# Batched top-k by token tile, tree sums, split low parts and wide late up blocks in a three-layer expert network

## The chip, the cores and the metric

The kernel runs on one NeuronCore of a Trainium2 chip. The metric is the device time of one execution in microseconds (us): 3051.55 is the median of three runs of the kernel before (3051.2 to 3052.03). TensorE (PE) multiplies matrices, VectorE (DVE) and ScalarE (ACT) work elementwise, GpSimd (POOL) and SyncE (SP) here mostly start DMAs. Each engine runs its own instructions in a fixed order and waits on semaphores.

## What is computed

256 tokens of width 1024 pass three blocks. Each block has a mixer (convolution and a recurrence; chunked linear attention; stick-breaking attention) and then an expert layer, `peer_ffn`, which takes most of the time and is what the change touches:

```
q = (xb @ w_q).reshape(TOK_BLOCK, PEER_HEADS, 2, PEER_DHALF)
s = jnp.einsum('thcd,hcnd->thcn', q, sub_keys).astype(jnp.float32)
top_s, top_i = lax.top_k(s, K)                       # K = 16 of 128 keys, 8 heads x 2 halves
cand = top_s[:, :, 0, :, None] + top_s[:, :, 1, None, :]
best_s, best_c = lax.top_k(cand.reshape(TOK_BLOCK, PEER_HEADS, K * K), K)
i1 = jnp.take_along_axis(top_i[:, :, 0], best_c // K, axis=-1)
i2 = jnp.take_along_axis(top_i[:, :, 1], best_c % K, axis=-1)
e = (i1 * PEER_NKEYS + i2).reshape(TOK_BLOCK, PEER_HEADS * K)
gate = jax.nn.softmax(best_s, axis=-1).reshape(TOK_BLOCK, PEER_HEADS * K)
u = expert_u[e]
act = jax.nn.gelu(jnp.einsum('td,ted->te', xb, u), approximate=False)
coef = (gate * act.astype(jnp.float32)).astype(xb.dtype)
return jnp.einsum('te,ted->td', coef, expert_v[e])
```

## The kernel before

The kernel gathers no experts. It computes the activation of all 16384 experts for all tokens ("up"), multiplies by a dense matrix of gates that is zero for experts not chosen, and multiplies by all of `expert_v` ("down"). Both loops run over 128 blocks of 128 experts.

**Weights in two parts.** `stream` (L72) loads a 128x1024 fp32 block into `raw` (four buffers), ScalarE makes `hi`, its value in the matmul format (L79), VectorE makes `lo = raw - hi` (L81); three buffers each of `hi` and `lo`. `mm3` (L109) multiplies as hi x hi, hi x lo, lo x hi, three matmuls for one product. The activations are stored in two parts as well, `xh` and `xl`, in two tiles.

**`peer` (L1049), one layer.** First the query loop: 16 blocks of `wq`, each with its scores (L1158) against the keys, which ScalarE copies into `S`. Then the up loop (L1189): a block is 8 x `mm3`, 24 matmuls of 256 columns into the PSUM tile `pu`, of which there are four, and a Gelu by ScalarE into the SBUF tile `C` (L1197). Then the down loop (`vstep`, L1208): 12 matmuls of 512 columns a block, with `ch` and `cl`, the two parts of `C` times gate.

**Work in the background.** The top-k of the scores, mostly VectorE's, is written as a generator (`background`, L1082) that yields its declared cost after each piece; `pull(rate)` (L1143), called once per query block from the third on and once per up block, takes pieces for a budget of 1.5. Before the change the pieces come in this order: rankings of all 32 score rows (`topk1`, both token tiles by turns), `topk2` of token tile 0 for its eight heads (rank the sums of the two halves, Exp, decode the rank into two indices, look up with 16 compare-and-multiply steps and four reduces, L1293 and L1300), 128 indirect DMAs that write tile 0's gates to the DRAM tensor `G` (L1097), `topk2` of tile 1, and the spread: for each four tokens of tile 1 VectorE and ScalarE build one-hot rows `A` and `B`, and eight recorded matmuls (L1131) make their dense gates `pg`, which multiply `C`. Gates for up blocks not yet done are put into `C` first, and the Gelu's result is then multiplied in (L1201).

**Buffers.** The scratch of the top-k lies in the last part of `C` (from block NS on). Tag "A" of the pool `wp` has two buffers: the one-hot tile `A` of the spread, then the tile `gate` of the down loop, into which POOL reads tile 0's gates from `G` for four blocks at a time (L1211); VectorE multiplies them into `C` (L1214).

**Order.** A scheduler in the framework orders each engine's instructions from the program text and dependencies; `issue_after` (L100, L1143) keeps an instruction behind a given `lo`.

Of the kernel before, what the change touches and what calls it, by code (L numbers as in the profile page):

```python
# [6 lines left out]
F32 = mybir.dt.float32  # L7
# [32 lines left out]
class Net:  # L40
# [31 lines left out]
    def stream(self, ap, n=1024):  # L72
# [7 lines left out]
        with self.behind():  # L80
            self.los.append(nc.vector.tensor_tensor(lo, raw, hi.bitcast(F32), op=OP.subtract))  # L81
# [172 lines left out]
    def block1(self, a, xh_out, xl_out, stop=None):  # L254
# [5 lines left out]
        with ExitStack() as ctx:  # L260
# [7 lines left out]
            xh = self.xp.tile([128, 8, 272], F32R, tag="xh", name="xh1")  # L268
            xl = self.xp.tile([128, 8, 272], F32R, tag="xl", name="xl1")
# [779 lines left out]
    def peer(self, xh, xl, wq, skT, uT, v, G, Gnext=None, rate=1.5, dve_a=2):  # L1049
# [7 lines left out]
        NS = 88  # L1057
        with ExitStack() as ctx:
# [9 lines left out]
            tmp = scr(1024, 5120)  # L1068
            small = [scr(1920, 6144 + 1920 * i) for i in range(2)]
            cand = [scr(512, 512 * i) for i in range(2)]  # L1070
            eq = scr(4096, 1024)
# [10 lines left out]
            def background():  # L1082
                for g in range(16):
                    for tt in range(2):
                        yield from self.topk1(views[tt], S[tt], tmp, 2 * g + tt)
                yield from self.topk2(views[0], cand[0], tmp, eq)
                pick = views[0]["pick"]
                idx = wp.tile([128, 128], U32, tag="idx", name="idx", bufs=1)
                gts = wp.tile([128, 128], F32, tag="gts", name="gts", bufs=1)
                V.tensor_copy(gts, pick[:, 2])  # L1090
                V.tensor_scalar(pick[:, 0], pick[:, 0], 128.0, self.col, op0=OP.mult, op1=OP.add)
                V.scalar_tensor_tensor(pick[:, 0], pick[:, 1], 16384.0, pick[:, 0], op0=OP.mult, op1=OP.add)
                V.tensor_copy(idx, pick[:, 0])
                for h in range(8):
                    now = []
                    for k in range(16 * h, 16 * h + 16):
                        i = nc.gpsimd.indirect_dma_start(  # L1097
                            G, bass.IndirectOffsetOnAxis(ap=idx[:, k:k + 1], axis=0), gts[:, k:k + 1], None,
                            compute_op=OP.add)
                        for j in now:  # L1100
                            tc.declare_no_dep(i.ins, j.ins, reason="distinct experts of a head")
# [333 lines left out]
```

## Time and profile before

| | |
|---|---|
| median of 3 runs | 3051.55 us |
| profiled execution | 3049.45 us, its span 3047.6 us |
| PE busy | 2973.8 us, 98% |
| DVE busy | 2077.3 us, 68% |
| ACT busy | 1619.5 us, 53% |
| POOL busy | 865.6 us, 28% |
| DMA | 568.80 MB, mean 187 GB/s |

The span runs from the first to the last instruction; 1.85 us lie around it. The up loops begin at 346, 1308 and 2278 us and the down loops at 750, 1713 and 2684 us; each down loop takes 348 us. What stands between is the mixers and the query loops. A share over the whole span hides the stages, so the rows further down are taken by stretch.

### The profile page before, as it was taken

How to read it: one execution, taken by the hardware profiler on the slowest of the kernel's cores; microseconds unless marked ns; L12 is line 12 of the kernel's file. 1: busy time of each engine (PE TensorE's matmuls, PEld its weight loads, DVE VectorE, ACT ScalarE, POOL GpSimd, SP SyncE). 2: the span in 40 equal slices, each digit the busy share in tenths (PEclk: the TensorE clock that was granted, in tenths of full speed). 3: DMA queues.
4: the chain of work that ended last, by engine and by line, in shares of the span. 5: the costliest groups of instructions: out<-in, count | busy, mean ns of one | idle time of the engine just before them, and what ended most of it. 6: DMA issues, size and time to landing. Idle time of an engine off the chain costs nothing.

```text
span 3047.6 us, 55671 instructions
## 1 busy us (share of the span) xinstructions
PE 2973.8 (98%) x21313; PEld 2719.7 (89%) x21313; DVE 2077.3 (68%) x4439; ACT 1619.5 (53%) x3016; POOL 865.6 (28%) x564
## 2 busy tenths in 40 slices
PE   9999999999999999999999999998999999999998
PEld 8888999999888888899999988887889999988886
DVE  6976997545666665798744566665599864466666
ACT  6345558544444454456844544446544774454443
POOL 0000057784000010008788100000002777800000
PEclk9999999999999999999999999999999999999999
DMA  9735566666676653456666666664345666666665
GB/s 312 238 131 202 174 167 139 167 184 194 217 218 218 217 185 118 157 175 158 138 182 183 204 218 217 218 214 164 119 156 173 151 147 185 182 215 217 216 217 177
DMA packets 231915, 568.80 MB, mean 187 GB/s; under 512 B 74416, under 2 KB 99264, under 8 KB 231392
## 3 DMA queue, kind: packets, MB, share of 16 engines
q1 hardware_dynamic: 165536, 529.31, 53.4%
q0 software_dynamic: 66112, 35.94, 8.3%
q8 instruction: 167, 2.74, 0.4%
q14 instruction: 100, 0.82, 0.1%
HBM read 533.49 MB, written 31.65 MB: 185 GB/s over the span
## 4 chain that ended last, share of the span: by engine, by line
PE 87%; DVE 9%; ACT 2%; issue 1%; DMA 1%; POOL 0%; DVEq 0%; ACTq 0%; SPq 0%; POOLq 0%
PE pu L113 11%; PE py L164 11%; PE py L162 11%; PE py L163 11%; PE pu L112 11%; PE pu L111 11%; PE pg L1131 3%; DVE lo L81 2%; PE pz L113 2%; PE pz L111 2%; PE pz L112 2%; DVE acc L340 1%; PE pq L113 1%; PE pq L112 1%; PE pq L111 1%
## 5 line engine op out<-in xcount | busy, mean ns | idle before, releaser
L81 DVE TENSOR_TENSOR lo<-raw,hi 128x1024 fp32r<-128x1024 f32 (+1 forms) x939 | 1142.6, 1218 | 762.6 <-ACT hi L79 757.3
L79 ACT CAST hi<-raw 128x1024 fp32r<-128x1024 f32 (+1 forms) x939 | 979.9, 1045 | 1192.5 <-issue 725.7
L1097 POOL DMA_INDIRECT G<-gts,idx x384 | 782.3, 2037 | 532.0 <-DVE gts L1090 236.3
L113 PE MATMUL pu<-xh,lo 128*128 128x256 f32 x3072 | 873.9, 284 | 7.7 <-DVE lo L81 7.7
L111 PE MATMUL pu<-xh,hi 128*128 128x256 f32 x3072 | 878.3, 286 | 3.0 <-ACT hi L79 3.0
L112 PE MATMUL pu<-xl,hi 128*128 128x256 f32 x3072 | 870.5, 283 | 0.0
L113 PEld LDWEIGHTS pu<-xh,lo 128*128 128x128 f32 x3072 | 590.2, 192 | 12.4 <-DVE lo L81 11.0
L162 PE MATMUL py<-hi,ch 128*128 128x512 f32 x1536 | 598.0, 390 | 0.0
L163 PE MATMUL py<-lo,ch 128*128 128x512 f32 x1536 | 597.1, 389 | 0.0
L164 PE MATMUL py<-hi,cl 128*128 128x512 f32 x1536 | 597.0, 389 | 0.0
L111 PEld LDWEIGHTS pu<-xh,hi 128*128 128x128 f32 x3072 | 590.3, 192 | 3.6 <-ACT hi L79 3.6
L112 PEld LDWEIGHTS pu<-xl,hi 128*128 128x128 f32 x3072 | 590.5, 192 | 0.0
L162 PEld LDWEIGHTS py<-hi,ch 128*128 128x128 f32 x1536 | 288.3, 188 | 61.4 <-ACT ch L106 1.9
L164 PEld LDWEIGHTS py<-hi,cl 128*128 128x128 f32 x1536 | 288.3, 188 | 61.1 <-DVE cl L107 1.4
L163 PEld LDWEIGHTS py<-lo,ch 128*128 128x128 f32 x1536 | 288.3, 188 | 59.5
L1211 POOL DMA_DIRECT2D gate<-G x96 | 51.9, 541 | 993.1 <-DVE C L1214 971.1
L107 DVE TENSOR_TENSOR cl<-C,ch 128x256 fp32r<-128x256 f32 x384 | 160.9, 419 | 4.4 <-ACT ch L106 4.4
L106 ACT CAST ch<-C 128x256 fp32r<-128x256 f32 x384 | 152.7, 398 | 12.9 <-DVE C L1214 12.9
L111 PE MATMUL pz<-xh,hi 128*128 128x256 f32 (+1 forms) x504 | 150.9, 301 | 7.9 <-ACT hi L79 5.5
L113 PE MATMUL pz<-xh,lo 128*128 128x256 f32 (+1 forms) x504 | 148.8, 296 | 1.0 <-DVE lo L81 1.0
L112 PE MATMUL pz<-xl,hi 128*128 128x256 f32 (+1 forms) x504 | 148.1, 294 | 0.1
L1197 ACT ACTIVATE C<-pu 128x128 f32<-128x128 f32 (+13 forms) x384 | 119.3, 312 | 0.2
(490 smaller groups left out, 3546.7 us busy)
## 6 DMA issues: line engine op xcount, KB each, us to landing
raw<-in_u_dram SPq DMA_DIRECT2D x384, 512.0 KB
raw<-in_v_dram SPq DMA_DIRECT2D x384, 512.0 KB
G<-zero SPq DMA_DIRECT2D x96, 256.0 KB
raw<-in_wq_dram SPq DMA_DIRECT2D x48, 512.0 KB
gate<-G POOLq DMA_DIRECT2D x96, 256.0 KB
raw<-in_w_in_dram SPq DMA_DIRECT2D x38, 512.0 KB
raw<-in_a_w_inT_dram SPq DMA_DIRECT2D x14, 512.0 KB
raw<-in_b_wT_dram SPq DMA_DIRECT2D x14, 512.0 KB
```

The source lines that it names most:

```text
L79: nc.scalar.copy(hi, raw)
L81: self.los.append(nc.vector.tensor_tensor(lo, raw, hi.bitcast(F32), op=OP.subtract))
L106: nc.scalar.copy(hi, src)
L107: nc.vector.tensor_tensor(lo, src, hi.bitcast(F32), op=OP.subtract)
L111: mm(out, lh, rh, start=start, stop=False)
L112: mm(out, lh, rl, start=False, stop=False)
L113: mm(out, ll, rh, start=False, stop=stop)
L162: mm(po[q], xh[:, ts], hi[:, h], start=f, stop=False)
L163: mm(po[q], xh[:, ts], lo[:, h], start=False, stop=False)
L164: mm(po[q], xl[:, ts], hi[:, h], start=False, stop=l)
L1097: i = nc.gpsimd.indirect_dma_start(G, bass.IndirectOffsetOnAxis(ap=idx[:, k:k + 1], axis=0), gts[:, k:k + 1], None, compute_op=OP.add)
L1197: nc.scalar.activation(C3[:, b, :tm], pa[:, :tm], AF.Gelu)
```

## The change

Five edits, all but the fourth inside `peer` and its helpers.

1. Top-k by token tile and by batches of four heads. `background` becomes two lists of jobs; each has the number of score rows that it needs, and `pull` takes the first list whose head may run, tile 0's before tile 1's. `topk2` runs on four heads and is called four times a layer; the scatter goes out in two halves; the scratch is smaller and starts at block 84 in place of 88.
2. In `topk2` the 16 lookup products are summed by a tree of adds in place of the reduces.
3. After the last job, up blocks take `hi` against both parts of x in one 512-column matmul, then `lo` against `xh`. The two halves of the PSUM tile are then added: ScalarE copies one out into a tile `sum` (tag "A"), VectorE adds the other, and the Gelus read `sum`.
4. `lo` is made in two halves of 512 elements, in every stream.
5. For that `xh` and `xl` become one tile with both parts of a chunk side by side.

```diff
--- before.py
+++ after.py
@@ -78,7 +78,10 @@
         lo = self.sp.tile([128, n], F32R, tag="lo", name="lo")
         nc.scalar.copy(hi, raw)
         with self.behind():
-            self.los.append(nc.vector.tensor_tensor(lo, raw, hi.bitcast(F32), op=OP.subtract))
+            for i in range(0, n, 512):
+                p = slice(i, min(i + 512, n))
+                sub = nc.vector.tensor_tensor(lo[:, p], raw[:, p], hi[:, p].bitcast(F32), op=OP.subtract)
+            self.los.append(sub)
         return hi, lo
 
     def chore(self, n):
@@ -265,8 +268,8 @@
                 s = VO1[name]
                 return vec[:, s] if i is None else vec[:, s.start + i:s.start + i + 1]
 
-            xh = self.xp.tile([128, 8, 272], F32R, tag="xh", name="xh1")
...
+    def peer(self, xh, xl, xx, wq, skT, uT, v, G, Gnext=None, rate=1.5, dve_a=2):
...
-        NS = 88
+        NS = 84
...
+            def scatter(hf):
+                K = slice(64 * hf, 64 * hf + 64)
...
+                for h in range(4 * hf, 4 * hf + 4):
...
+            jobs = [[], []]
+            for tt in range(2):
+                for hf in range(2):
+                    for g in range(8 * hf, 8 * hf + 8):
+                        jobs[tt].append((g + 1, self.topk1(views[tt], S[tt], tmp, 2 * g + tt)))
+                    jobs[tt].append((8 * hf + 8, self.topk2(views[tt], cand, tmp, eq, 4 * hf)))
+                    if tt == 0:
+                        jobs[tt].append((8 * hf + 8, scatter(hf)))
+            jobs[1].append((16, spread()))
+            debt, now_ = [0.0], [None]
+
+            def pull(budget, scored=16):
...
                 debt[0] += budget
                 with tc.issue_after(self.los[-PACE].ins):
                     while debt[0] > 0:
-                        c = next(bg, None)
+                        if now_[0] is None:
+                            q = next((q for q in jobs if q and q[0][0] <= scored), None)
+                            if q is None:
+                                debt[0] = 0.0
+                                return
+                            now_[0] = q.pop(0)[1]
+                        c = next(now_[0], None)
                         if c is None:
-                            return False
-                        debt[0] -= c
-                return True
+                            now_[0] = None
+                        else:
+                            debt[0] -= c
...
                 if g > 1:
-                    pull(rate)
+                    pull(rate, g - 1)
...
-                for c in range(8):
-                    s = slice(c * 128, c * 128 + 128)
-                    self.mm3(pa[:, :256], hi[:, s], lo[:, s], xh[:, c], xl[:, c], c == 0, c == 7)
+                src = pa
+                if any(jobs) or now_[0]:
+                    for c in range(8):
+                        s = slice(c * 128, c * 128 + 128)
+                        self.mm3(pa[:, :256], hi[:, s], lo[:, s], xh[:, c], xl[:, c], c == 0, c == 7)
+                else:
+
+                    for c in range(8):
+                        s = slice(c * 128, c * 128 + 128)
+                        nc.tensor.matmul(pa, hi[:, s], xx[:, c].rearrange("p x n -> p (x n)"), start=c == 0, stop=False)
+                    for c in range(8):
+                        s = slice(c * 128, c * 128 + 128)
+                        nc.tensor.matmul(pa[:, 256:], lo[:, s], xh[:, c], start=False, stop=c == 7)
+                    src = wp.tile([128, 256], F32, tag="A", name="sum")
+                    nc.scalar.copy(src, pa[:, 256:])
+                    with tc.issue_after(self.los[-1].ins):
+                        V.tensor_tensor(src, src, pa[:, :256], op=OP.add)
                 tm = state["tok"]
-                nc.scalar.activation(C3[:, b, :tm], pa[:, :tm], AF.Gelu)
+                nc.scalar.activation(C3[:, b, :tm], src[:, :tm], AF.Gelu)
...
-        for h in range(8):
+        for h in range(4):
...
         for j in range(16):
-            V.scalar_tensor_tensor(r16(e2[:, j]), r16(cf.rearrange("p c n -> p (c n)")), float(j),
-                                   tj[:, :, j, None].to_broadcast([128, 16, 16]), op0=OP.is_equal, op1=OP.mult)
+            V.scalar_tensor_tensor(e[:, j], cfn, float(j), tj[:, :, j, None].to_broadcast([128, 8, 16]),
+                                   op0=OP.is_equal, op1=OP.mult)
...
-        for i in range(4):
-            N = slice(i * 64, i * 64 + 64)
-            V.tensor_reduce(pick[:, 0:2].rearrange("p c n -> p (c n)")[:, N], e3[:, N], axis=AX.X, op=OP.add)
-            yield 1.1
...
+        for n in (1024, 512, 256):
+            V.tensor_tensor(eq[:, :n], eq[:, :n], eq[:, n:2 * n], op=OP.add)
+            if n > 256:
+                yield 0.0012 * n
+        V.tensor_tensor(pick[:, 0:2], eq[:, 0:128].rearrange("p (c n) -> p c n", c=2),
+                        eq[:, 128:256].rearrange("p (c n) -> p c n", c=2), op=OP.add)
```

Three places show how the engines' orders move. Numbers behind a name tell one buffer from another; a block's `raw`, `hi`, `lo` and `pu` carry near numbers.

TensorE at the end of the first layer's up loop, before: the last matmuls of block 127 and the first of down.

```order
L112 MATMUL pu_9849<-xl_97,hi_9845 128x256
L113 MATMUL pu_9849<-xh_96,lo_9846 128x256
L111 MATMUL pu_9849<-xh_96,hi_9845 128x256
L112 MATMUL pu_9849<-xl_97,hi_9845 128x256
L113 MATMUL pu_9849<-xh_96,lo_9846 128x256
L162 MATMUL py_9878<-hi_9886,ch_9891 128x512
L163 MATMUL py_9878<-lo_9887,ch_9891 128x512
L164 MATMUL py_9878<-hi_9886,cl_9892 128x512
```

The same place now, the last three up blocks:

```order
L1224 MATMUL pu_9780<-x_96,hi_9775 128x512 x8
L1227 MATMUL pu_9780<-x_96,lo_9776 128x256 x8
L1224 MATMUL pu_9811<-x_96,hi_9806 128x512 x8
L1227 MATMUL pu_9811<-x_96,lo_9807 128x256 x8
L1224 MATMUL pu_9842<-x_96,hi_9837 128x512 x8
L1227 MATMUL pu_9842<-x_96,lo_9838 128x256 x8
L165 MATMUL py_9866<-hi_9874,ch_9880 128x512
L166 MATMUL py_9866<-lo_9875,ch_9880 128x512
L167 MATMUL py_9866<-hi_9874,cl_9881 128x512
```

A block is now eight wide matmuls on `hi` and then eight narrow ones on `lo`, where 24 narrow ones went round `hi`, `hi`, `lo`. Of the 128 blocks of each layer, 74 keep the old form and 54 have the new one; the first of these follows the last `pg` matmul of the spread.

ScalarE at the same place, before, from the `hi` of block 127 on:

```order
L79 CAST hi_9845<-raw_9843 128x1024
L1197 ACTIVATE C_3873<-pu_9744 128x128
L1200 ACTIVATE act_9770<-pu_9744 128x128
L79 CAST hi_9886<-raw_9884 128x1024
L1197 ACTIVATE C_3873<-pu_9779 128x128
L1200 ACTIVATE act_9805<-pu_9779 128x128
L106 CAST ch_9891<-C_3873 128x256
L79 CAST hi_9909<-raw_9907 128x1024
L1197 ACTIVATE C_3873<-pu_9814 128x128
L1200 ACTIVATE act_9840<-pu_9814 128x128
L106 CAST ch_9914<-C_3873 128x256
L1197 ACTIVATE C_3873<-pu_9849 128x128
```

and now, from the `hi` of the first down block on:

```order
L79 CAST hi_9874<-raw_9872 128x1024
L1229 COPY sum_9797<-pu_9780 128x256
L1233 ACTIVATE C_3925<-sum_9797 128x128
L1236 ACTIVATE act_9801<-sum_9797 128x128
L79 CAST hi_9898<-raw_9896 128x1024
L1229 COPY sum_9828<-pu_9811 128x256
L1233 ACTIVATE C_3925<-sum_9828 128x128
L1236 ACTIVATE act_9832<-sum_9828 128x128
L79 CAST hi_9922<-raw_9920 128x1024
L1229 COPY sum_9859<-pu_9842 128x256
L1233 ACTIVATE C_3925<-sum_9859 128x128
L1236 ACTIVATE act_9863<-sum_9859 128x128
```

Each block's two Gelus now stand behind a copy and read `sum`, which VectorE has to add up first; `hi` of the block three further on stands ahead of a block's Gelus in both.

VectorE in the same stretch, before:

```order
L81 TENSOR_TENSOR lo_9846<-raw_9843,hi_9845 128x1024
L1201 TENSOR_TENSOR C_3873<-C_3873,act_9770 128x128
L81 TENSOR_TENSOR lo_9887<-raw_9884,hi_9886 128x1024
L1201 TENSOR_TENSOR C_3873<-C_3873,act_9805 128x128
L1214 TENSOR_TENSOR C_3873<-C_3873,gate_9882 128x128
L107 TENSOR_TENSOR cl_9892<-C_3873,ch_9891 128x256
L81 TENSOR_TENSOR lo_9910<-raw_9907,hi_9909 128x1024
L1201 TENSOR_TENSOR C_3873<-C_3873,act_9840 128x128
L1214 TENSOR_TENSOR C_3873<-C_3873,gate_9882 128x128
L107 TENSOR_TENSOR cl_9915<-C_3873,ch_9914 128x256
```

and now:

```order
L83 TENSOR_TENSOR lo_9899<-raw_9896,hi_9898 128x512
L1231 TENSOR_TENSOR sum_9828<-sum_9828,pu_9811 128x256
L83 TENSOR_TENSOR lo_9899<-raw_9896,hi_9898 128x512
L1237 TENSOR_TENSOR C_3925<-C_3925,act_9832 128x128
L83 TENSOR_TENSOR lo_9923<-raw_9920,hi_9922 128x512
L1231 TENSOR_TENSOR sum_9859<-sum_9859,pu_9842 128x256
L83 TENSOR_TENSOR lo_9923<-raw_9920,hi_9922 128x512
L1237 TENSOR_TENSOR C_3925<-C_3925,act_9863 128x128
L1250 TENSOR_TENSOR C_3925<-C_3925,gate_9870 128x128 x3
L110 TENSOR_TENSOR cl_9881<-C_3925,ch_9880 128x256
L110 TENSOR_TENSOR cl_9905<-C_3925,ch_9904 128x256
L110 TENSOR_TENSOR cl_9929<-C_3925,ch_9928 128x256
```

The add into `sum` stands between the two halves of a later block's `lo`. The multiplies by `gate` used to alternate with the last multiplies by `act`; now three of them stand behind all of these, with three `cl` after them. The DMA that fills `gate_9870` takes a buffer of tag "A", in which `sum` was before.

## Rows read from the trace of the kernel before

**Rows 1.** The page's part 1: busy us, share of the span, instructions.
```profile
PE 2973.8 (98%) x21313; PEld 2719.7 (89%) x21313; DVE 2077.3 (68%) x4439; ACT 1619.5 (53%) x3016; POOL 865.6 (28%) x564
```

**Rows 2.** Busy us (x instructions) of PE, PEld, DVE, ACT, POOL; granted clock; DMA.
```profile
560.00:747.00 187.00, 187.00 (x1561) 187.00 (x1560) 92.85 (x132) 89.48 (x195) 137.94 (x59) 1.00 0.67 186
760.00:1095.00 335.00, 335.00 (x1478) 276.87 (x1477) 217.07 (x370) 166.53 (x247) 15.80 (x30) 1.00 0.69 216
```

**Rows 3.** The same view, first up block to first gate matmul, three layers.
```profile
346.20:451.30 105.10, 101.07 (x827) 99.42 (x826) 101.59 (x322) 53.81 (x83) 38.74 (x21) 1.00 0.63 177
1307.60:1414.40 106.80, 103.45 (x828) 101.15 (x827) 103.21 (x330) 53.87 (x84) 38.48 (x19) 0.98 0.61 177
2277.50:2385.00 107.50, 104.14 (x831) 101.70 (x830) 103.94 (x331) 54.40 (x85) 38.54 (x19) 0.98 0.61 177
```

**Rows 4.** VectorE's groups by shape: count | busy us, mean ns | idle before.
```profile
L107 DVE TENSOR_TENSOR cl<-C,ch 128x256 fp32r<-128x256 f32 x384 | 160.9, 419 | 4.4 <-ACT ch L106 4.4
L1214 DVE TENSOR_TENSOR C<-C,gate 128x128 f32<-128x128 f32 x384 | 109.3, 285 | 0.0
L1293 DVE SCALAR_TENSOR_TENSOR C<-C 128x256 f32<-128x256 f32 x96 | 33.7, 418 | 0.2
```

**Rows 5.** VectorE in order of time, lookup sums: start us, us, instruction.
```profile
1395.76 1.22 DVE L81 TENSOR_TENSOR lo<-raw,hi 128x1024 fp32r<-128x1024 f32 x1
1396.90 1.98 DVE L1300 TENSOR_REDUCE C<-C 128x64 f32<-128x1024 f32 x1
1398.80 1.22 DVE L81 TENSOR_TENSOR lo<-raw,hi 128x1024 fp32r<-128x1024 f32 x1
```

**Rows 6.** ScalarE in order of time at the second Exp of layer 2.
```profile
1374.74 1.05 ACT L79 CAST hi<-raw 128x1024 fp32r<-128x1024 f32 x1 [1.55 <-PE pu L112]
...
1376.09 1.28 ACT L1270 ACT_TABLE_LOAD   x1
1381.34 0.31 ACT L1270 ACTIVATE C<-C 128x128 f32<-128x128 f32 x1 [3.96 <-DVE C L1269]
1381.66 1.28 ACT L1197 ACT_TABLE_LOAD   x1
```

**Rows 7.** ScalarE in order of time, one late up block of layer 1.
```profile
741.83 1.05 ACT L79 CAST hi<-raw 128x1024 fp32r<-128x1024 f32 x1 [1.49 <-PE pu L112]
742.78 0.27 ACT L1197 ACTIVATE C<-pu 128x128 f32<-128x128 f32 x1
742.95 0.27 ACT L1200 ACTIVATE act<-pu 128x128 f32<-128x128 f32 x1
```

**Rows 8.** TensorE in order of time where up ends, layer 1.
```profile
750.27 0.28 PE L113 MATMUL pu<-xh,lo 128*128 128x256 f32 x1
750.39 0.40 PE L162 MATMUL py<-hi,ch 128*128 128x512 f32 x1
```

**Rows 9.** POOL in order of time: the last add to G, the first gates.
```profile
719.94 2.57 POOL L1097 DMA_INDIRECT G<-gts,idx  x1 [0.30 <-issue]
727.00 1.20 POOL L1211 DMA_DIRECT2D gate<-G  x2 [4.49 <-DVE lo L81]
756.48 0.54 POOL L1211 DMA_DIRECT2D gate<-G  x1 [28.28 <-DVE C L1214]
```

**Rows 10.** POOL in order of time where one head's writes follow another's.
```profile
437.47 1.54 POOL L1097 DMA_INDIRECT G<-gts,idx  x1 [0.31 <-issue]
441.82 1.54 POOL L1097 DMA_INDIRECT G<-gts,idx  x1 [2.81 <-issue]
```

**Rows 11.** Busy by stretch around TensorE's wait that ends at 2082.32.
```profile
2080.00:2083.20 3.20, 0.87 (x6) 0.63 (x7) 3.20 (x6) 0.96 (x3) 0.53 (x1) 1.00 0.76 234
2083.40:2086.60 3.20, 3.08 (x14) 2.58 (x13) 3.20 (x8) 0.79 (x2) 0.35 (x1) 0.50 0.95 334
```

**Rows 12.** TensorE's waits: us in total, times, longest.
```profile
PE ptr L199 <- DVE res L722: 12.4, 5, 3.4
...
PE pz L113 <- DVE lo L81: 5.3, 3, 2.3
```

More of the change, by code (lines that the diff above doesn't have):

```diff
@@ L1067, in peer @@
             S = [scr(2048, 2048 * i).rearrange("p (g n) -> p g n", n=128) for i in range(2)]
[L1068 to L1071, printed above, removed]
+            tmp = scr(1024, 4096)
+            small = [scr(1920, 5120 + 1920 * i) for i in range(2)]
+            eq = scr(2048, 8960)
+            cand = scr(256, 11008)
             views = [self.topk_views(s_) for s_ in small]
@@ L1080, in after, with gates @@
                     tc.add_manual_dep(i.ins, j.ins.name, SYNC, reason="adds of the head before")
[L1082 to L1093, printed above, removed]
-                for h in range(8):
[L1095 to L1101, printed above, removed]
-                        after(i)
-                        now.append(i)
-                    last[:] = now
-                yield 0.8
-                yield from self.topk2(views[1], cand[1], tmp, eq)
-                pick = views[1]["pick"]
-                pt = self.ps.tile([128, 512], F32, tag="y", name="pt", bufs=4)
-                for i in range(3):
-                    nc.tensor.transpose(pt[:, i * 128:i * 128 + 128], pick[:, i], self.ident)
-                idT = wp.tile([128, 5, 128], F32, tag="idT", name="idT", bufs=1)
-                nc.scalar.copy(idT[:, 0:3].rearrange("p a b -> p (a b)"), pt[:, :384])
-                V.tensor_scalar(idT[:, 3], idT[:, 0], -1.0, None, op0=OP.mult)
-                V.tensor_scalar(idT[:, 4], idT[:, 2], -1.0, None, op0=OP.mult)
-                yield 1.0
+            def gates():
                 for t0 in range(252, 127, -4):
@@ new lines, in spread @@
+            def spread():
+                pick = views[1]["pick"]
+                pt = self.ps.tile([128, 512], F32, tag="y", name="pt", bufs=4)
+                for i in range(3):
+                    nc.tensor.transpose(pt[:, i * 128:i * 128 + 128], pick[:, i], self.ident)
+                nc.scalar.copy(idT[:, 0:3].rearrange("p a b -> p (a b)"), pt[:, :384])
+                V.tensor_scalar(idT[:, 3], idT[:, 0], -1.0, None, op0=OP.mult)
+                V.tensor_scalar(idT[:, 4], idT[:, 2], -1.0, None, op0=OP.mult)
+                yield 1.0
+                yield from gates()
@@ L1261, in topk2 @@
             V.tensor_tensor(c3[:, :, o:o + n * nb].rearrange("p h (a b) -> p h a b", b=nb),
[L1262 to L1265 removed]
+                            tv4[:, :, 0, a0:a1, None].to_broadcast([128, 4, n, nb]),
+                            tv4[:, :, 1, None, 0:nb].to_broadcast([128, 4, n, nb]), op=OP.add)
+        yield 0.9
+        for h in range(4):
             self.top16(bv[:, h], bi[:, h], c3[:, h], tmp[:, h * 64:h * 64 + 64])
@@ L1390, in xt @@
         def xt():
-            return [n.xp.tile([128, 8, 256], F32R, tag="x" + x, name="x" + x) for x in "hl"]
+            t = n.xp.tile([128, 8, 2, 256], F32R, tag="x", name="x")
+            return t[:, :, 0], t[:, :, 1], t
         def peer(l, x):
```

83 lines of the change are left out of this document (48 added, 35 removed).

## The prediction

> **What bounds the kernel now.** I read the page's busy table first: TensorE is busy for 98% of the span, VectorE for 68% [rows 1]. Then stretches with one kind of work. In the late up stretch 1561 matmuls of 256 columns fill 187 us, 119.8 ns each; in the down stretch 1478 of 512 columns fill 335 us, 226.7 ns each [rows 2]. A column at the full clock (2.4 GHz) takes 0.4167 ns, so 256 and 512 columns are 106.7 and 213.3 ns, and both kinds carry the same 13 ns on top: a fixed price per matmul. There TensorE never waits.
>
> It does wait early in each up loop, while VectorE does the top-k. The three stretches from the first up matmul to the first matmul of the gate spread last 105.1, 106.8 and 107.5 us with 827, 828 and 831 matmuls [rows 3]. At 119.8 ns these are 99.1, 99.2 and 99.6 us, so 6.0, 7.6 and 7.9 us are lost: 21.5 us in all. VectorE is busy there for 97% of the time.
>
> Two things lose them. VectorE's starts show what an instruction really occupies: a `lo` of 1024 elements 1.14 us (1395.76 to 1396.90) though its record says 1.22, a reduce of L1300 1.90 us [rows 5]; a record is some 0.083 longer than the step to the next start. A reduce and a `lo` come to 3.04 us, against a block of 24 x 0.1198 = 2.875 us. And the Exp of the second top-k keeps ScalarE from 1376.09, when its table load starts, to 1381.65, of which 3.96 us waiting for VectorE, and a second table load follows; no `hi` is made meanwhile [rows 6].
>
> **The change part by part.** *Late up blocks.* From the first block after the spread, 54 of 128 blocks of each layer, 162 in all, replace 24 matmuls of 256 columns by 8 of 512 and 8 of 256. The columns stay 6144. 8 x 226.7 + 8 x 119.8 = 2772 ns against 2875: 0.103 us less per block, **-16.7 us** for 162.
>
> The Trainium skill (TensorE: Matmul & The Clock Gate, "Back-to-back issue gap") gives N/2.4 + 2.5 ns at the full clock. By that rule eight matmuls fewer are worth an estimated 20 ns a block, 3.2 us in all. The trace disagrees: 13 ns each.
>
> *What the wide blocks add.* A ScalarE copy out of PSUM (0.4 us), a VectorE add (0.42 us, as the 256-element L107 [rows 4]), and a longer way round: ScalarE makes `hi` of block b+3, copies b, waits for the add of b, does two Gelus; VectorE does the first half of `lo` of b+3, the add, the second half. In that order ScalarE's round is `hi` 1.05, first half of `lo` 0.60 (half of 1.14 plus half of the fixed part), add 0.42, Gelus 0.17 each by their starts (742.78, 742.95) [rows 7], hops about 0.1: 2.5 us. That is below 2.77, so TensorE stays the bound and this costs nothing; `hi` is two blocks early, so a slower round would first eat some 5 us of lead per layer.
>
> *Top-k.* The 48 rankings of a layer stay. By starts, lookups were 32 of 256 elements (0.335 us) and 8 reduces (1.90): 25.9 us; now 64 of 128 (0.20) and trees of 1024, 512, 256 and 128 elements, 4 times (1.14 + 0.60 + 0.34 + 0.20): 21.9 us. The small steps at half length, twice as often, give about 4 us back: a fixed 0.07 us each [rows 4, 5]. In the up stretches VectorE's busy time, 101.6 to 103.9 us, less 35 `lo` of 1.14 leaves 62 to 64 us of this background [rows 3], 1.77 us per block or more. The rate of 1.5 per block against declared costs (72.8 a layer before, 86.4 now) hands the work out in 49 portions before (14 in the query loop, 35 up blocks) and 58 now (14 and 44). So the layer's background is 49 x 1.77 = 86 us, before and, by the two sums just made, still. Per portion with its `lo`: before 1.77 + 1.14 = 2.91 us, over the block's 2.875; now 86/58 + 1.20 = 2.68, under it. Late then: the Exp. There are four a layer, one in the query loop, three in the up loop (before two). With VectorE under its limit each should find it about one `lo` behind, a delay that the two-block lead takes up. Bounds: all 21.5 us go; or each of three Exps costs what the worst costs now (some 3.7 us by the arithmetic of rows 3 and 6, where 7.6 us hold two), 11 per layer, +12. I take **-13**: a little remains at each Exp and at the start of the spread, which looks the same in both orders.
>
> The spread starts eight or nine blocks later; it is 32 x 8 matmuls wherever it stands: nothing.
>
> *Where up hands over to down.* Before, the first down matmul starts 0.12 us after the last up matmul [rows 8], since the first gate pair was read long before. Now the buffers of tag A hold the sums of up blocks to the end: `gate` of the first down blocks takes the buffer of block 126's sum, and POOL waits for its last Gelu. That one is over 1.85 us after block 126 ends (copy, half a `lo`, add, two Gelus), 0.9 us before 127 ends. Then comes the gate's issue, 0.54 us [rows 9], and its landing. No row shows a gate's landing; the nearest are POOL's writes to G, where a new head started 4.35 us after the start of the issue before it, 2.81 us after its end [rows 10]. So 3.35 us, then the multiply (0.29) and the cast `ch` (0.4) with hops: TensorE stands still for about 3.4 us. Behind that multiply VectorE holds two more, three `cl` and the next `lo`, all for down; POOL holds only the next gate, wanted four blocks later. (G itself is long written: its last add was issued at 719.94 [rows 9], and the first half now goes out earlier, for which nobody waits.) After a wait of 3.4 us [rows 12] TensorE's next 3.2 us ran at a granted 0.50, the 1.2 GHz level [rows 11]; that takes another 1.7 us. **+15.3 us** for three layers (5.1 each). Bounds: a landing at 2 us and no slow stretch, 2.1 each, +6; a landing at 5 us and twice the slow stretch, 8.5 each, +25.
>
> *`lo` in halves elsewhere.* VectorE pays one fixed part more, 0.07 us for each of 939; in the down loop it is busy 65% [rows 2], so there is room. In the mixers the first half arrives 0.6 us earlier for the few matmuls that wait for it (5.3 us in three waits [rows 12]), and chains queued behind a `lo` get 0.07 later. **-1**, bounds -3 and +4.
>
> Sum: -16.7 - 13 + 15.3 - 1 = -15.4. The profiled execution is 3049.45 us (span 3047.6, 1.85 around it), giving 3034.0; it lies 2.1 below the median of the runs, 3051.55, so for timed runs I say **3036 us**.
>
> **Rivals.**
> (A) Hand-over eats it: a stall of 8 us a layer and little won in top-k: -16.7 - 1 + 25 - 5 = +2, 3054 at its worst, about 3050 in its middle. For it: rows 11 show slow stretches after every wait of that length; against: the stall's parts are short rows.
> (B) The 13 ns go with columns, not with matmuls: a wide one then takes 2 x 119.8 ns, and eight fewer bring nothing: 0 - 13 + 15.3 - 1 = +1, 3053. Against: rows 2, where 512 columns take 226.7 ns, not 239.6. By the rule of the Trainium skill cited above this rival would be near the truth, at 3.2 us won and 3050.
> (C) Slower: ScalarE's round in the wide blocks is longer than TensorE's 2.77. A round of r us costs (r - 2.77) x 54 - 5.5 us a layer; from r = 2.97 this outweighs the 5.1 won per layer. No row shows an add with a PSUM operand or these hops. At r = 3.15 it costs 45 us: 3081. Against: my sum is 2.5, and rows 7 leave ScalarE idle 1.49 us a block.
> (D) Slower: each Exp stalls as the worst does: -16.7 + 12 + 15.3 - 1 = +10, 3061. For it: three events instead of two; against: 0.2 us of slack a block.
> (E) Better: gate lands almost in time and all top-k waits go: -16.7 - 21.5 + 3 - 1 = -36, 3015.
> That wide blocks hardly occur is excluded: 162 stand in TensorE's order.
>
> **How the numbers follow.** Forecast 0.64, A 0.12, B 0.05, C 0.05, D 0.04, E 0.10. The forecast alone spans 3026 to 3045. Adding E's upper part and A's and B's middle: 3021 to 3050, leaving out the rest of E, C and D. A measurement tells 0.2%, 6 us, from no change. Faster by more: nearly all of the forecast, E, a little of A and B: 0.75. Within: 0.14. Slower: C, D and A's end: 0.11.
>
> **What would show it.** Late up blocks at a step of 2.77 us with 16 matmuls and no waits prove the first term; a step above 2.87 with ScalarE or VectorE as releaser proves C. Up to the spread, matmul count x 119.8 ns against the stretch gives what top-k still costs; VectorE waits for `hi` should appear there. At the hand-over I expect three TensorE waits of 3 to 4 us before py L165, released by `ch`, with POOL's gate issue released by ScalarE just before, and a stretch at granted 0.5 behind each. If py follows pu without a gap, that term is wrong; if up blocks 0 to 43 still lose 6 to 8 us a layer, the second is.

## The result and the profile after

The changed kernel takes 3031.36 us (median of five runs, 3028.37 to 3038.28) against 3051.55 in the same comparison (3047.97 to 3052.14): a ratio of 0.994, with a 95% interval of 0.9925 to 0.9954. The forecast was 3036. The profiled execution takes 3028.37 us with a span of 3026.6, so 21.0 us less span than before.

The page's busy line of the changed kernel answers to [rows 1]: 1296 matmuls fewer (162 blocks of eight), and VectorE and ScalarE busier.

```profile
PE 2946.5 (97%) x20017; PEld 2644.4 (87%) x20017; DVE 2205.2 (73%) x5779; ACT 1713.5 (57%) x3165; POOL 770.7 (25%) x564
```

The stretches from the first up matmul to the first of the spread, three layers of the changed kernel (us, then busy us and count of PE, PEld, DVE, ACT, POOL, granted clock, DMA), answer to [rows 3]:

```profile
341.60:469.88 128.28, 128.20 (x1069) 127.80 (x1067) 120.96 (x492) 70.09 (x107) 102.35 (x48) 1.00 0.73 189
1299.59:1427.88 128.29, 128.21 (x1069) 127.82 (x1067) 121.35 (x493) 69.96 (x107) 97.63 (x48) 1.00 0.74 190
2262.63:2391.08 128.45, 128.22 (x1068) 127.82 (x1066) 121.44 (x493) 70.13 (x107) 101.33 (x48) 1.00 0.72 190
```

Reckoned as in the forecast, 1069 matmuls at 119.8 ns are 128.07 us: 0.2, 0.2 and 0.5 us are lost where 6 to 8 were. (The view's count takes in some matmuls that only reach into a stretch; by starts there are 1065, 240 more than before.) The stretches are longer only because the spread begins ten blocks later.

The late blocks, ScalarE and then VectorE of the changed kernel in order of time (start, duration, both us), answer to [rows 7]:

```profile
729.05 1.05 ACT L79 CAST hi<-raw 128x1024 fp32r<-128x1024 f32 x1
730.06 0.37 ACT L1229 COPY sum<-pu 128x256 f32<-128x256 f32 x1
731.19 0.31 ACT L1233 ACTIVATE C<-sum 128x128 f32<-128x128 f32 x1 [0.76 <-DVE sum L1231]
731.41 0.30 ACT L1236 ACTIVATE act<-sum 128x128 f32<-128x128 f32 x1
731.84 1.05 ACT L79 CAST hi<-raw 128x1024 fp32r<-128x1024 f32 x1
```

```profile
730.13 0.69 DVE L83 TENSOR_TENSOR lo<-raw,hi 128x512 fp32r<-128x512 f32 x1 [0.90 <-ACT hi L79]
730.74 0.41 DVE L1231 TENSOR_TENSOR sum<-sum,pu 128x256 f32<-128x256 f32 x1
731.07 0.68 DVE L83 TENSOR_TENSOR lo<-raw,hi 128x512 fp32r<-128x512 f32 x1
```

The order is the forecast one: first half, add, second half. ScalarE goes round in 2.66 us (729.05 to 731.71), 0.16 more than forecast, and then has 0.13 us left before the next `hi`. So TensorE is still the bound, and its own order shows the step of a block (TensorE, one wide block of the changed kernel and the beginning of the next):

```profile
727.01 2.00 PE L1224 MATMUL pu<-x,hi 128*128 128x512 f32 x8
728.85 1.11 PE L1227 MATMUL pu<-x,lo 128*128 128x256 f32 x8
729.80 0.40 PE L1224 MATMUL pu<-x,hi 128*128 128x512 f32 x1
```

From 727.01 to 729.80 are 2.79 us, where the forecast had 2.772. The mean over 48 blocks is 2.793. A block in the old form takes 2.880, start to start, in the kernel before. The narrow half takes 0.95 us, 0.01 less than eight narrow steps; the wide half takes 1.84 where eight steps of 226.7 ns are 1.81.

Where up hands over to down, all engines of the changed kernel in order of time, from ScalarE's last Gelu of block 126 on; the bracket is the idle time before and what ended it. It answers to [rows 8, 9].

```profile
734.20 0.29 ACT L1236 ACTIVATE act<-sum 128x128 f32<-128x128 f32 x1
734.44 1.11 PE L1227 MATMUL pu<-x,lo 128*128 128x256 f32 x8
...
734.79 0.62 POOL L1247 DMA_DIRECT2D gate<-G  x1 [100.32 <-PE pu L1224]
...
738.90 0.70 DVE L1250 TENSOR_TENSOR C<-C,gate 128x128 f32<-128x128 f32 x3 [1.30 <-DMA gate<-G]
739.23 1.02 ACT L109 CAST ch<-C 128x256 fp32r<-128x256 f32 x3 [1.95 <-DVE C L1250]
...
739.68 0.50 PE L165 MATMUL py<-hi,ch 128*128 128x512 f32 x1 [4.14 <-ACT ch L109]
```

POOL starts the first gate 0.30 us after that Gelu ends (734.49), though the bracket names a matmul as the releaser: an instruction waits for several semaphores, and the engine named had long been free. VectorE's multiply starts 4.11 us after the issue, and TensorE stands for 4.14 us; in the other two layers it is 4.65 and 4.79 us from the issue, and TensorE stands for 4.68 and 4.82. The waits of all three layers and, as an answer to [rows 12], the largest that was there before:

```profile
PE py L165 <- ACT ch L109: 13.6, 3, 4.8
PE ptr L202 <- DVE res L725: 11.9, 5, 3.3
```

Two stretches of the changed kernel around it (columns as above) answer to [rows 11]: the wait, and what follows it at a granted 0.58 of the full clock, most of it at the 1.2 GHz level.

```profile
735.60:739.60 4.00, 0.00 (x0) 0.00 (x0) 2.58 (x7) 1.30 (x6) 0.58 (x1) 1.00 0.83 267
739.70:743.10 3.40, 3.40 (x9) 2.66 (x10) 1.06 (x3) 0.55 (x2) 0.00 (x0) 0.58 0.33 134
```

Where the 21.0 us come from, by the starts of the first and last matmul of each stage in the two traces:

| stage, three layers | before | after | difference | forecast |
|---|---|---|---|---|
| up loops | 1215.8 | 1181.2 | -34.6 | -29.7 |
| last up to first down matmul | 0.4 | 14.5 | +14.1 | } +15.3 |
| down loops | 1045.6 | 1051.0 | +5.4 | } |
| query loops, mixers, ends | 785.8 | 780.0 | -5.8 | -1 |

### The profile page after: what moved, and what is told of

Read it like the earlier page. It is cut to its first block, busy times and chain, and to the rows that moved or that the text cites. A ratio compares the mean times of both kernels' runs of the same rounds, so it can differ in the third digit from the quotient of the medians.

```text
span 3026.6 us, 55004 instructions
## 1 busy us (share of the span) xinstructions
PE 2946.5 (97%) x20017; PEld 2644.4 (87%) x20017; DVE 2205.2 (73%) x5779; ACT 1713.5 (57%) x3165; POOL 770.7 (25%) x564
## 4 chain that ended last, share of the span: by engine, by line
PE 89%; DVE 5%; ACT 2%; DMA 2%; issue 1%; SPq 0%; POOL 0%; DVEq 0%; ACTq 0%; POOLq 0%
PE py L165 11%; PE py L167 11%; PE py L166 11%; PE pu L1224 10%; PE pu L115 7%; PE pu L114 7%; PE pu L116 7%; PE pu L1227 5%; PE pg L1101 3%; PE pz L116 2%; PE pz L114 2%; PE pz L115 2%; DVE lo L83 1%; PE pq L116 1%; PE pq L115 1%
## 5 line engine op out<-in xcount | busy, mean ns | idle before, releaser
L83 DVE TENSOR_TENSOR lo<-raw,hi 128x512 fp32r<-128x512 f32 (+1 forms) x1877 | 1256.4, 684 | 618.0 <-ACT hi L79 616.5
L1124 POOL DMA_INDIRECT G<-gts,idx x384 | 686.3, 1787 | 367.9 <-issue 146.8
L114 PE MATMUL pu<-x,hi 128*128 128x256 f32 x1776 | 510.2, 287 | 0.0
L116 PE MATMUL pu<-x,lo 128*128 128x256 f32 x1776 | 502.6, 283 | 0.0
L115 PE MATMUL pu<-x,hi 128*128 128x256 f32 x1776 | 502.4, 283 | 0.0
L115 PEld LDWEIGHTS pu<-x,hi 128*128 128x128 f32 x1776 | 340.6, 192 | 0.0
L114 PEld LDWEIGHTS pu<-x,hi 128*128 128x128 f32 x1776 | 340.3, 192 | 0.0
L116 PEld LDWEIGHTS pu<-x,lo 128*128 128x128 f32 x1776 | 340.1, 192 | 0.0
L1224 PE MATMUL pu<-x,hi 128*128 128x512 f32 x1296 | 324.5, 392 | 0.0
L1224 PEld LDWEIGHTS pu<-x,hi 128*128 128x128 f32 x1296 | 233.1, 189 | 41.7
L1227 PEld LDWEIGHTS pu<-x,lo 128*128 128x128 f32 x1296 | 176.8, 190 | 12.6
L1227 PE MATMUL pu<-x,lo 128*128 128x256 f32 x1296 | 180.7, 282 | 0.0
```

The costliest lines, as they stand in the source:

```text
L83: sub = nc.vector.tensor_tensor(lo[:, p], raw[:, p], hi[:, p].bitcast(F32), op=OP.subtract)
L114: mm(out, lh, rh, start=start, stop=False)
L115: mm(out, lh, rl, start=False, stop=False)
L116: mm(out, ll, rh, start=False, stop=stop)
L1124: i = nc.gpsimd.indirect_dma_start(G, bass.IndirectOffsetOnAxis(ap=idx[:, k:k + 1], axis=0), gts[:, k:k + 1], None, compute_op=OP.add)
L1224: nc.tensor.matmul(pa, hi[:, s], xx[:, c].rearrange("p x n -> p (x n)"), start=c == 0, stop=False)
```

## Experiments

All times are medians of runs taken together with the kernel before, whose median was 3051.58 to 3053.07 us in them. None of these kernels leaves anything out.

### The buffers of the sum (own_tag)

```
-                    src = wp.tile([128, 256], F32, tag="A", name="sum")
+                    src = wp.tile([128, 256], F32, tag="act", name="sum")
```

> The changed kernel with one word different: `sum` shares its buffers with `act` instead of with `A` and `gate`. Theory (the shared buffers make the stall): the first loads of `gate` are again issued in the up stage, so the wait between the last up matmul and the first down matmul falls from 4.4, 5.0 and 5.1 us to 0.1 us in each layer, and the down loops return from 350.2, 350.7 and 350.1 us to about 348.4: 14.1 + 5.3 = 19.5 us less than the changed kernel, about 3012 us, 0.987 of the kernel before. Rival (the stall is the tail of the wide block itself: copy, sum, Gelu and the first split of the down stage, which follow each other whatever the buffers are): more than 2.5 us of each wait stays, and the time is 3022 us or more.

Measured: 3012.83 us, ratio 0.9872 (0.9857 to 0.9887). The waits are 0.12 us in each layer and the down loops 348.4 us. TensorE where up ends, and POOL's last add to `G` and first gates, 104 us before up ends:

```profile
740.64 0.76 PE L1227 MATMUL pu<-x,lo 128*128 128x256 f32 x5
741.24 0.40 PE L165 MATMUL py<-hi,ch 128*128 128x512 f32 x1
```

```profile
631.56 1.59 POOL L1124 DMA_INDIRECT G<-gts,idx  x1 [0.31 <-issue]
636.91 1.19 POOL L1247 DMA_DIRECT2D gate<-G  x2 [3.76 <-DVE sum L1231]
```

So the shared buffers made the whole of the hand-over's price, the slow stretch included. The tail of the wide block costs nothing by itself.

### No wide blocks (no_wide)

```
-                if any(jobs) or now_[0]:
+                if True:
```

> The changed kernel with every up block in the old form (24 matmuls of 256 columns, no `sum`). If the two parts of the wide form are as the traces say, its gain of 13.3 us goes (each late block 2.875 instead of 2.793 us) and its stall of 19.5 us goes with it: about 3025 us, 0.991 of the kernel before and faster than the changed kernel. The waits of top-k stay away (0.2 us lost in 128.3 us). Rival (the stall is not the wide form's but comes from the lookups or the halves): the waits between up and down stay at 4 to 5 us and the time is about 3044 us. Rival (the wide form gains the forecast 16.7 us in full and the 3.4 us missing lie elsewhere): up stages longer than those of the changed kernel by 16 us or more.

Measured: 3027.15 us, ratio 0.9915 (0.9902 to 0.9929). In its trace the waits before down are 0.12 us, and the late stage, from the last gate matmul to the last up matmul, is 158.38 us in each layer, 153.71 with wide blocks: 4.67 less, 14.0 us in three layers. The first up matmul after the gates and the last one, layer 1 of no_wide, then of the changed kernel (158.35 and 153.68 us apart):

```profile
588.23 0.36 PE L114 MATMUL pu<-x,hi 128*128 128x256 f32 x1
746.58 0.28 PE L116 MATMUL pu<-x,lo 128*128 128x256 f32 x1
```

```profile
581.59 0.36 PE L114 MATMUL pu<-x,hi 128*128 128x256 f32 x1
735.27 0.28 PE L1227 MATMUL pu<-x,lo 128*128 128x256 f32 x1
```

So the wide form brings 14.0 us and, in the buffers of `A`, costs 19.5. On the whole the third edit made the changed kernel no faster: the two ratios differ by 0.0025 in favour of the kernel without it, and the intervals overlap a little.

### What took the waits of top-k away

Five kernels bear on this. The first keeps the changed top-k but has `lo` in one piece (whole_lo):

```
-            for i in range(0, n, 512):
-                p = slice(i, min(i + 512, n))
-                sub = nc.vector.tensor_tensor(lo[:, p], raw[:, p], hi[:, p].bitcast(F32), op=OP.subtract)
-            self.los.append(sub)
+            self.los.append(nc.vector.tensor_tensor(lo, raw, hi.bitcast(F32), op=OP.subtract))
```

> The changed kernel with each low part again in one subtraction of 1024 columns. Theory (the halves don't matter to top-k, since the lookups' long additions are what was in the way): the stretches of top-k lose under 1 us each as now. Rival (the halves let VectorE's queue through between the pieces): 5 us or more per layer of the 21.5 lost before come back, 3046 us or more. Of the mixers and query loops, which became 5.9 us shorter by the changed trace: if the halves did that, it goes back and the time is about 3037; if it is the new order of the work around them, 3031.

Measured: 3043.98 us, ratio 0.9972 (0.9963 to 0.9981). Nothing is lost in top-k. Neither of the times expected came: the hand-over got worse, 7.4, 7.5 and 5.4 us from the last up to the first down matmul, since the add now stands behind a whole `lo`, and with it the Gelu and the gate's issue. TensorE's waits there in this kernel:

```profile
PE py L162 <- ACT ch L106: 19.4, 3, 7.2
```

The issue comes 1.6 us later against the end of up in each layer, and the gate's first use 5.5, 5.5 and 3.5 us after it instead of 4.1 to 4.8. Waits and down loops are 6.9 us more than in the changed kernel by the traces. The other 5.7 of the 12.6 us between the medians are not located: the traces have 3.3 us in query loops, mixers and ends, and this one has 91 us at a granted 0.5, that of the changed kernel 74. With the 6.9 us of the hand-over the first of the two times expected, 3037, would be 3044, so it is not excluded that a share of the halves was lost here (see *Halves elsewhere* below).

The second is the kernel before with its background in smaller portions (rate125):

```
-    def peer(self, xh, xl, wq, skT, uT, v, G, Gnext=None, rate=1.5, dve_a=2):
+    def peer(self, xh, xl, wq, skT, uT, v, G, Gnext=None, rate=1.25, dve_a=2):
```

> The kernel before with one number changed: VectorE's side work is handed out at 1.25 per block instead of 1.5, which spreads it over 58 instead of 49 portions, as many as the changed kernel has. Theory (smaller portions): the 21.5 us that TensorE lost in top-k (6.0, 7.6 and 7.9) fall to under 4 in all, about 3032 us, 0.994. Rival (trees: single long additions of 1.9 us are what made `lo` late, and they are still here): at least 4 us lost in each layer, 3045 us or more. The end of the side work moves from block 74 or so to about 89 of 128, which no matmul waits for by either.

Measured: 3041.69 us, ratio 0.9962 (0.9948 to 0.9976). The up stretches of this kernel, long reduces and all:

```profile
348.80:476.97 128.17, 128.17 (x1068) 127.80 (x1066) 118.13 (x355) 67.42 (x104) 42.61 (x21) 1.00 0.66 185
1306.25:1434.43 128.18, 128.18 (x1069) 127.82 (x1067) 119.08 (x362) 67.44 (x104) 43.26 (x21) 1.00 0.66 186
2268.97:2397.13 128.16, 128.16 (x1068) 127.80 (x1067) 119.29 (x364) 67.42 (x104) 43.20 (x21) 1.00 0.66 186
```

Nearly all of the 21 us lost in top-k are gone by this one number. The expected 3032 did not come, because in layer 3 POOL, which starts tile 0's adds to `G` later at this rate, was not done when down began. That takes 9.5 us with the slow stretch behind it (POOL of this kernel; TensorE waits 7.7 us for what follows):

```profile
2667.60 1.55 POOL L1097 DMA_INDIRECT G<-gts,idx  x1 [0.30 <-issue]
2671.26 1.20 POOL L1211 DMA_DIRECT2D gate<-G  x2 [2.11 <-DMA G<-gts,idx]
```

The third is own_tag with large portions (rate176):

```
-    def peer(self, xh, xl, xx, wq, skT, uT, v, G, Gnext=None, rate=1.5, dve_a=2):
+    def peer(self, xh, xl, xx, wq, skT, uT, v, G, Gnext=None, rate=1.76, dve_a=2):
```

> The changed kernel with `sum` in the buffers of `act` (as in own_tag) and the rate at 1.76 instead of 1.5, so that the changed top-k, with its trees and four Exps, comes in 49 portions as that of the kernel before did. Theory (it is the size of a portion that made TensorE wait): by 86 us / 49 + 1.20 = 2.96 us a portion is again over the block's 2.875, and 3 to 8 us are lost per layer between the first up matmul and the first of the spread; some 26 more wide blocks win back 2.3 us; 3020 to 3034 us, slower than own_tag's 3012.8. Rival (trees alone do it, since they take long instructions out of VectorE's queue): under 1 us lost per layer, 3010 to 3012 us.

Measured: 3026.11 us, ratio 0.99 (0.9882 to 0.9919). It loses 4.9, 4.7 and 2.1 us in the stretches of top-k. The time and two of the layers are as the theory of portions has it; the third lies under its 3 to 8 us, and the sum of 11.7 is less than the 21 of before.

The fourth is the changed kernel with reduces in place of the trees (reduces):

```
+        e3 = eq.rearrange("p (j n) -> p n j", j=16)
+        for i in range(2):
+            V.tensor_reduce(pick[:, i], e3[:, i * 64:i * 64 + 64], axis=AX.X, op=OP.add)
+            yield (1.2288, 0.6144)[i]
```

> The changed kernel with each tree of four additions replaced by two reductions of 16 x 64 elements (1.2 us or so each), the declared costs and so the 58 portions kept. Theory (portions): the stretches from the first up matmul to the spread still lose under 1 us per layer, and the time is that of the changed kernel, 3031 us within 5. Rival (the trees are what frees VectorE): 3 us or more lost per layer, 3040 us or more.

Measured: 3045.72 us, ratio 0.9968 (0.9954 to 0.9982). The theory of portions alone falls here: 12 us are lost with the portions kept. The reduces take 2.0 us each, not the 1.2 expected (VectorE's groups by shape, layer 1 of this kernel; count, busy us, mean ns):

```profile
L1337 DVE TENSOR_REDUCE C<-C 128x64 f32<-128x1024 f32 x7 | 14.0, 1997 | 0.0
```

The fifth kernel is the one before with the halves alone, the edit of whole_lo the other way (halves_only):

> The kernel before with nothing changed but each low part in halves. Theory (halves help only where TensorE waits for a first `lo`, in the mixers and query loops): 3 to 6 us there, 3046 to 3048 us, and 5 us or more per layer still lost in top-k. Rival (halves let top-k's queue through): the 21.5 us lost in top-k fall below 10, 3037 us or less. Rival (nothing but a reshuffle): 3051 within 2.

Measured: 3053.46 us, ratio 0.9999 (0.999 to 1.0009). Top-k loses more than before, 27 us: that halves make it worse no theory had. The time fits the last rival, since the kernel before had 3052.56 in this comparison.

One quantity puts all in line: how long VectorE's records are per block of 24 matmuls in these stretches (busy DVE over a twenty-fourth of the count of PE), against what TensorE loses there (length less count x 119.8 ns), sums over three layers. The rows of one more kernel, middle layer of halves_only, and of reduces:

```profile
1308.10:1417.03 108.93, 104.37 (x829) 101.27 (x827) 105.85 (x368) 53.95 (x84) 39.65 (x19) 0.98 0.61 172
```

```profile
1308.89:1441.21 132.32, 130.32 (x1069) 128.31 (x1067) 127.62 (x487) 69.57 (x106) 100.07 (x52) 1.00 0.73 183
```

| kernel | top-k | portions | `lo` | DVE per block, us | lost, us |
|---|---|---|---|---|---|
| whole_lo | trees | 59 | whole | 2.65 | 0.4 |
| rate125 | reduces | 59 | whole | 2.67 | 0.6 |
| after | trees | 59 | halves | 2.72 | 0.9 |
| reduces | reduces | 59 | halves | 2.86 | 12.0 |
| rate176 | trees | 50 | halves | 2.90 | 11.7 |
| before | reduces | 49 | whole | 2.98 | 21.3 |
| halves_only | reduces | 49 | halves | 3.05 | 27.2 |

The portions are counted to the one that brings the first gates, by the costs declared in the code; the forecast and the expectations have 58 for 59 and 49 for the 50 of rate176. A block is 2.88 us. At 2.72 and below next to nothing is lost; from 2.86 on 12 us are, and each further 0.1 us costs 8 us or so over three layers. (VectorE is not busy without a gap even then, 127.62 of 132.32 us in the row of reduces, so the knee lies somewhat under a block's time.) The last two columns hang together by themselves once VectorE is full, since the stretch is then as long as its work; what shows the cause is that each change of the load alone moves the loss: the rate (before and rate125), the trees (after and reduces), the halves (before and halves_only). Smaller portions, trees and whole `lo`s are three ways to the same end. Halves work against it.

### The missing 3 us of the wide blocks (interleave)

own_tag with wide and narrow matmuls by turns:

```
                     for c in range(8):
                         s = slice(c * 128, c * 128 + 128)
                         nc.tensor.matmul(pa, hi[:, s], xx[:, c].rearrange("p x n -> p (x n)"), start=c == 0, stop=False)
-                    for c in range(8):
-                        s = slice(c * 128, c * 128 + 128)
                         nc.tensor.matmul(pa[:, 256:], lo[:, s], xh[:, c], start=False, stop=c == 7)
```

> own_tag with the wide block's order changed: wide matmul and narrow matmul alternate over c, where all eight wide ones came first. The late block took 2.793 us instead of the 2.772 of eight wide and eight narrow steps; the excess stands in the first five wide ones. Theory (something else that runs at a block's beginning, the copy out of PSUM or the add that reads it, slows them): it stays near 2.79 us a block, late stage 153.7 us, 3012.8 us. Rival (the switch between narrow and wide costs, at each switch): 15 switches instead of 1, some 10 ns or more each, so 2.9 us or more a block and 3030 us or more. If the excess goes, 2.77 us a block, 3009 us.

Measured: 3017.41 us, ratio 0.9884 (0.9865 to 0.9903); late stage 155.51 us. TensorE of this kernel:

```profile
727.02 0.40 PE L1224 MATMUL pu<-x,hi 128*128 128x512 f32 x1
727.26 0.28 PE L1225 MATMUL pu<-x,lo 128*128 128x256 f32 x1
727.37 0.40 PE L1224 MATMUL pu<-x,hi 128*128 128x512 f32 x1
727.61 0.28 PE L1225 MATMUL pu<-x,lo 128*128 128x256 f32 x1
```

Means of 49 blocks: 236.7 ns after a wide matmul and 116.7 after a narrow one, the same for all eight pairs, so 353.3 a pair against 226.7 + 120.0 = 346.7. The block takes 2.827 us, less than the 2.9 expected by the second theory but more than 2.793. That the excess comes with every pair, wherever ScalarE's copy and VectorE's add fall, speaks against the first theory. The kernel before settles it, which has neither copy nor add. Where its up loop hands over to down, 256 columns are followed by 512 without a wait (TensorE of the kernel before, layer 1):

```profile
750.27 0.28 PE L113 MATMUL pu<-xh,lo 128*128 128x256 f32 x1
750.39 0.40 PE L162 MATMUL py<-hi,ch 128*128 128x512 f32 x1
...
751.55 0.39 PE L164 MATMUL py<-hi,cl 128*128 128x512 f32 x1
```

These five wide steps are 233, 236, 228, 233 and 230 ns (1.16 us in all, 26 ns more than five of 226.7), and the next are 227. A wide block of own_tag begins with the same five numbers within 2 ns; its first narrow step is 113 instead of 120. So a run of wide matmuls after narrow ones pays some 27 ns at its beginning, of which 7 come back at the change to narrow: 20 ns a block. By turns it is some 7 ns a pair, 53 ns a block. What in TensorE takes this time, no run shows.

### Wide blocks in the spread too (wide_spread, wide_spread3)

own_tag, with the flag set when the spread begins:

```
             def gates():
+                state["spread"] = True
-                if any(jobs) or now_[0]:
+                if "spread" not in state:
```

> own_tag with the wide form in the up blocks of the spread as well, 34 more per layer. Theory (VectorE and ScalarE have the room: by the busy times of the changed kernel's spread, 85.6 and 92.0 us in 111.7 us of 34 blocks, a copy and an add of 0.4 us each bring them to 2.9 and 3.1 us in a block of 3.2): 34 x 3 x 0.085 = 8.7 us less, 3004 us. Rival (with ScalarE above nine tenths, `hi` comes late as in top-k where VectorE is that full): it loses more than it wins, TensorE waits for `hi` in the spread, 3013 us or more.

Measured: 3008.26 us, ratio 0.9847 (0.9833 to 0.9861). The spread takes 109.6 us instead of 111.7 with no wait of TensorE: 2.1 us a layer, 6.3 in all. A layer has 84 wide blocks by its matmuls, 30 more than own_tag and not 34, so a block gains 70 ns where 85 were expected. The second kernel has `dve_a=3`:

> wide_spread with three of four one-hot rows of a spread step made on VectorE instead of two, which takes 0.8 us per step from ScalarE and gives VectorE 0.35 us. If ScalarE's load is what limits wide_spread, this one is faster than it; if wide_spread loses nothing there, this one is slower or the same, since VectorE goes to 3.2 us a block: 3004 to 3015 us.

Measured: 3007.03 us, ratio 0.9842 (0.9829 to 0.9856): no difference from wide_spread that can be told, so ScalarE was not the limit. (The declared cost of a spread step grows with `dve_a`, so the spread is also drawn out, from 109.6 to 126.3 us; the up loops take 391.5 us in both.) These two are the fastest kernels of the study.

## Why the prediction was right, term by term

*Late up blocks, -16.7.* Measured -14.1 by the step of a block (162 x 0.087 us), -14.0 against no_wide. The mechanism holds: a fixed price per matmul, of which there are eight fewer. Rival B, under which the wide form brings nothing, falls. The step that failed in size is "8 x 226.7 + 8 x 119.8 = 2772 ns": it took both prices from uniform stretches [rows 2], and a block that changes width pays 20 ns more. The price of the change stood in the trace of the kernel before, just behind [rows 8]. The 119.8 ns are a little low: the count in [rows 2] takes in the last gate matmuls, of 128 columns, and start to start a narrow matmul takes 120.0, so that an old block is 2.880 us and the forecast would have been -17.2. The Trainium skill (TensorE: Matmul & The Clock Gate, "Back-to-back issue gap") would have given an estimated 3.2 us by its 2.5 ns per matmul, a formula that it keeps for the isolated gap, adding that in a stream the weight loads count as well; the pair of kernels shows 14.0, so for this stream the measurement decides against the formula.

*What the wide blocks add, nothing.* Right: no wait stands in the late stage, and rival C falls. It was closer than forecast: a round of 2.66 us where 2.5 were worked out.

*Top-k, -13.* Measured -20.6 (34.6 less the 14.0 of the wide form). The comparison it rested on, 2.91 us of VectorE per block before and 2.68 after against 2.875, is what the seven kernels of the table bear out: 2.98 and 2.72 by the traces. "Two things lose them" does not hold as it stands: rate125 keeps each long reduce and each Exp and loses 0.6 us, so it was the load per block and no single instruction. The declared costs of the new top-k add up to 87.4 a layer in the code, not 86.4, which makes 59 portions and changes nothing else. The step that failed is "a little remains at each Exp and at the start of the spread": under the limit nothing remained, also with the third Exp. That the lead of two blocks takes up the late `hi` of an Exp fits this; no run was made on it alone. Rival D falls by this; the half of E on top-k came true.

*Hand-over, +15.3.* Measured +19.5: 14.1 in waits and 5.4 behind them. The place, the chain and the slow stretch were as forecast, and own_tag shows that the buffers were the cause. Mis-sized was the landing: 3.35 us from the issue by the nearest row [rows 10], while the first multiply came 4.11, 4.65 and 4.79 us after the issue began; TensorE's waits were 4.1 to 4.8 us instead of 3 to 4. The slow stretch was 1.8 us a layer, forecast 1.7. Rival A needed 8 us a layer; it was 6.5. Its "after every wait of that length" was read from one wait in [rows 11]; the trace of the kernel before has four of 3.2 to 3.5 us, and a slow stretch at or just behind each.

*Halves elsewhere, -1.* The traces differ by -5.8 us in query loops, mixers and ends, and one pair of traces cannot say whether the halves did this. own_tag runs the same code up to the first up block and its trace reaches the first query matmul at 293.60 us, the changed kernel's at 288.31. The two rows (changed kernel, then own_tag, from the start) differ in the granted clock:

```profile
0.00:288.31 288.31, 266.18 (x3548) 248.94 (x3549) 222.85 (x476) 146.06 (x233) 15.63 (x62) 0.98 0.69 228
```

```profile
0.00:293.60 293.60, 270.27 (x3548) 253.43 (x3549) 224.15 (x477) 145.38 (x233) 15.56 (x62) 0.96 0.68 224
```

The kernel before stood at 292.52. With the three mixers together, the same code took 599.2 us in one execution and 604.2 in the other; before had 602.7. Outside up loops, hand-overs and down loops the three kernels with whole `lo` have 785.8, 783.2 and 789.2 us (before, whole_lo, rate125), the other seven with halves at the rate of 1.5 783.0 to 789.4. So by the traces this term is 0 within 3 us, and of the 21.0 us up to 6 may be chance.

The medians say something else. Take the distance of a kernel's median from that of the kernel before, and from it what the two traces differ by in up loops, hand-overs and down loops. For the eight kernels with halves at the rate of 1.5, the changed one among them, -3.2 to -5.6 us are left; for whole_lo and rate125, whose `lo` is whole, +0.9 and +0.3. halves_only is the plainest: its up loops are 5.9 us longer, its median only 0.9. (rate176, with halves and query loops 5.9 us longer, has +1.1.) Since the stages are from one trace each, what the halves bring outside top-k stays open between 0 and -5.

The sum by mechanism is -14.0 - 20.6 + 19.5 = -15.1, which is the forecast -15.4 for partly wrong reasons: two terms were off by +3 and +4, one by -8, and that they nearly cancelled was luck. The medians differ by 20.2; the 5 us between the two are the open part just named, chance or halves.

## What to carry to other kernels

Before a new tile takes a buffer tag, ask which later tile of that tag is loaded ahead of time: here one word was worth 18.5 us, nearly as much as the whole change won. Background work handed out per block cost next to nothing here while its engine's time per block stayed some 0.15 us under the 2.88 us of TensorE's block, and 12 to 27 us once it came up to it or over it; compare these two numbers, rather than single long instructions. A price per matmul read from a uniform stretch leaves out what a change of width costs; look for a place in the trace where the width changes already.

## What the runs showed that was not expected

TensorE pays for a change between 256 and 512 columns, in the kernel before as well: 20 ns once a block with eight of each in a row, 53 ns with eight changes there and back.

All in all, a trace of these kernels holds 70 to 91 us at a granted 0.5, and two that run the same code up to the first query matmul differ there by 12 us of it (12 in the changed kernel, 25 in own_tag). Single runs of the changed kernel lie 10 us apart. So terms of a few us are to be read from stages, not from the total.

A gate of 256 KB, issued by POOL while its core's DMA was busy for 83%, took 4.11 us from issue to its first use; over the layers it was 4.1 to 4.8 us, and in whole_lo 3.5 to 5.5.
